# Low parts by negative copies and accumulating DMAs, and one plain tile fewer in each up-projection

## The chip, the cores and the metric

The kernel runs on one core of a Trainium2 chip. The metric is the device time in microseconds, the median of several runs; a profiled execution is read beside it. Lines are written L198 for line 198 of the kernel before.

## The reference

One layer on x of 512 tokens by 1024 channels, all in float32:

```
x = x + 0.5 * (silu(h @ w_gate) * (h @ w_up)) @ w_down      # h = rmsnorm(x), d_ff = 2816
x = x + mixer(rmsnorm(x))                                    # chunked attention and pooling
x = x + 0.5 * (silu(h @ w_gate) * (h @ w_up)) @ w_down      # second FFN, own weights
x = rmsnorm(x)
```

The change touches only the up-projections (gate and up) of the two FFNs.

## The kernel before

**Numbers in two parts.** Every float32 operand z is split into a high part, z rounded to the matmul's format (fp32r), and a low part z - high, which is rounded in its turn. `split` (L128) makes them: ScalarE copies (L132, or L135 with a scale), VectorE subtracts (L133, or L136 with a scale). A product is then three matmuls (`mm3`, L198 to L200): high by high, high weights by low tokens, low weights by high tokens. The third is the only one that reads the low part of the weights.

**The up-projection** (`ffn_up`) goes over 22 tiles of 128 hidden channels, gate and up each. It has three kinds of stages.

- The first stage takes tiles 0 and 1 together, over four chunks of weights, while the norm is still under way. At its end stands the norm's mean on TensorE (L334), then Ln and Exp on ScalarE, and two passes on VectorE (L324, L328) that give rb, the factor of each token.
- Plain tiles: 2 to PLAIN - 1. Each has two weight tiles of 128 by 1024 (`weights`, loads at L181 on SyncE's queue, split by `split`) and 2 x 8 `mm3` with 512 columns, 48 matmuls. `evacuate` (L418 gate times rb, L420 silu on ScalarE, L422, then L725 in `place` for up times that, and L732 and L733 in `sums` for every second one of a pair) empties the two banks. PLAIN is 5 in the first FFN and 4 in the second.
- Seven-product tiles: from PLAIN to 21. Tokens and weights are taken as 2 by 2 blocks, and the Winograd form of Strassen's scheme makes the tile from seven products of half the columns (4 `mm3` each, 84 matmuls with 256 columns), in the order A11, S3, S2, A22, S1, A12, S4 of the token operands. Their order on TensorE, VectorE and ScalarE is written out by hand. The weight operands are sums of blocks (L494, L500, L501), again in two parts (L471 and L476), called w11, w13, w24 and w22. S3 and A22 use halves of w13 and w24 (S and on), S2 the first half of w24, A12 and S4 w22.

**The way into the seven-product tiles.** The token operands have to exist by the first of these tiles. `Norm.blocks` gives a list of 19 pieces of work, which `piece` hands out: eight scalings of x by gain and rb (L359), sums of blocks (L365), and the splits: S3 and S2 (`whole`, with sign -1, so L135 and L136), S4 (`whole`, L132 and L133), and A11, A22, S1 and A12 (`halves`, two half operands each, 512 columns, into the rooms in which the norm's h lay, so only when the last plain tile has read them). The plain tiles before the last get four pieces after each weight tile; before the last one all but four pieces are handed out; the last plain tile gets the remaining four: A11 after its second step, A22 after the fourth, S1 after the sixth, and A12 at the end, after the evacuation. The last plain tile alternates between its two banks at every step and carries the preparation of the first seven-product tile in between. The order of plain tiles and pieces on TensorE, VectorE and ScalarE is a scheduler's, by readiness and then by place in the code.

**GpSimd's queue.** `Down.make_sums` copies one column of a given tile (mark, L714), which ties it to that tile's progress, and then issues DMAs in DRAM (L716, some of them accumulating) that make the weight sums of the down-projection. A region `manual_schedule` keeps the order of the instructions inside it on its engine; where a region falls among others is the scheduler's. In the second FFN, x is also put aside from here (L935).

**Rooms.** Parts of weights have four rooms in turn, raw weights two and two; a room is given again when its last reader is done.

Of the kernel before, what the change touches and what calls it, by code (L numbers as in the profile page):

```python
# [11 lines left out]
AF = mybir.ActivationFunctionType  # L12
ALU = mybir.AluOpType
# [3 lines left out]
P = 128  # L17
D = 1024
S = 512
KD = D // P  # L20
# [14 lines left out]
RAW = 2  # L35
HILO = 3
SHIFT = 16
PLAIN = (5, 4)
PROBS = 3
EARLY = 16  # L40
LATE = 4
# [4 lines left out]
    weights=(-1.0, 0.905, 3.0), qk=2.0, turn=1.1, head=0.9, pool=0.965, map=0.95, u=2.0,  # L46
# [10 lines left out]
def layer(  # L57
# [31 lines left out]
    nc = tc.nc  # L89
# [28 lines left out]
    A11, S1, S3, S2, A12, A22, S4 = range(7)  # L118
# [10 lines left out]
    def split(src, hi, lo, scale=None):  # L129

        if scale is None:
            nc.scalar.copy(hi, src)  # L132
            nc.vector.tensor_tensor(lo, src, hi.bitcast(F32), op=ALU.subtract)  # L133
        else:
            nc.scalar.activation(hi, src, AF.Copy, scale=scale)  # L135
            nc.vector.scalar_tensor_tensor(  # L136
                lo, src, scale, hi.bitcast(F32), op0=ALU.mult, op1=ALU.subtract
            )


    rooms: list = [(wpool, "raw", RAW, 1024)]
    n_raw = [0]

# [28 lines left out]

    n_own = [0]

    def weights(src, parts=1):
        n = src.shape[-1]
        raw = raw_tile()
        hi, lo = part_tiles()
        for i in range(parts):
            part = slice(i * n // parts, (i + 1) * n // parts)  # L180
            nc.sync.dma_start(raw[:, part], src[:, part])  # L181
            split(raw[:, part], hi[:, part], lo[:, part])
        return hi, lo

    def ordered(acc):
# [7 lines left out]
    def mm3(acc, a, b, start, stop, further=False):  # L193

        more = dict(skip_group_check=True) if further else {}
        acc = acc.rearrange("p (i a) -> p i a", a=2)
        high, low = (z.rearrange("p (a i) -> p i a", a=2) for z in b)
        nc.tensor.matmul(acc, a[0], high, start=start, stop=False, **more)  # L198
        nc.tensor.matmul(acc, a[0], low, start=False, stop=False, **more)  # L199
        nc.tensor.matmul(acc, a[1], high, start=False, stop=stop, **more)  # L200

    def cut(pair, lo, n):
        return pair[0][:, lo : lo + n], pair[1][:, lo : lo + n]
# [80 lines left out]
    class Norm:  # L284
# [57 lines left out]
        def blocks(self, pool, aside):  # L342

            x_lo, x_hi = (z[:, : 4 * S].rearrange("p (k c) -> p k c", c=S) for z in aside[:2])
            a11, a21 = x_lo[:, :, :HT], x_lo[:, :, HT:]  # L350
            a12, a22 = x_hi[:, :, :HT], x_hi[:, :, HT:]
            s2, s4, s1 = (
                z[:, at : at + 4 * HT].rearrange("p (k c) -> p k c", c=HT)
                for z, at in ((aside[0], 4 * S), (aside[1], 4 * S), (aside[2], 0))
            )
            self.a = [None] * 7

            def scale(k):
                nc.vector.scalar_tensor_tensor(  # L359
                    (x_lo, x_hi)[k // 4][:, k % 4], x[k], gain_sb[:, self.which, k : k + 1],  # L360
                    self.rb, op0=ALU.mult, op1=ALU.mult,
                )

            def add(dst, one, two, op):
                nc.vector.tensor_tensor(dst, one, two, op=op)  # L365

            def whole(i, src, make, sign=None):
                pair = [make().rearrange("p (k c) -> p k c", c=HT) for _ in range(2)]
                split(src, *pair, sign)
                self.a[i] = [[z[:, k] for k in range(4)] for z in pair]  # L370

            def halves(i, src):

                self.a[i] = [[], []]
                for k in (0, 2):
                    pair = [
                        hpool.tile([P, 2, HT], F32R, tag="h", name=name("ha")) for _ in range(2)
                    ]
                    split(src[:, k : k + 2], *pair)
                    for z, to in zip(pair, self.a[i]):  # L380
                        to.extend(z[:, j] for j in range(2))

            def by_x(i):
                return lambda: xpool.tile([P, 2 * S], F32R, tag=f"x{i.pop()}", name=name("xa"))

            def extra():
                z = pool.tile([P, 4 * HT + 64], F32R, tag="extra", name=name("sa"), bufs=2)
                return z[:, 48 : 48 + 4 * HT]

            free = [3, 2, 1, 0]  # L390
            return [(scale, k) for k in range(KD)] + [
                (add, s1, a21, a22, ALU.subtract),
                (add, s2, s1, a11, ALU.add),
                (add, a21, a11, a21, ALU.add),
                (whole, S3, a21, by_x(free), -1.0),
                (whole, S2, s2, by_x(free), -1.0),
                (add, s4, s2, a12, ALU.subtract),
                (whole, S4, s4, extra),
                (halves, A11, a11),
                (halves, A22, a22),  # L400
                (halves, S1, s1),
                (halves, A12, a12),
            ]


    def ffn_up(norm, wA, down, loaded, in_order, plain, turns=()):
# [9 lines left out]
        def evacuate(f, gate, up):  # L416
            g = temp()
            nc.vector.tensor_tensor(natural(g), ordered(gate), natural(norm.rb), op=ALU.mult)  # L418
            sg = temp()
            nc.scalar.activation(sg, g, AF.Silu)  # L420

            nc.vector.tensor_tensor(sg, sg, norm.rb, op=ALU.mult)  # L422
            down.place(f, ordered(up), sg)
            down.sums(f)
            return sg
# [89 lines left out]
        def low24(n):  # L515
            if n < KF:
                low((n, 24))

        for n, f in enumerate(down.order[2 : plain - 1], 2):
            banks = []  # L520
            for j in range(2):
                wj = weights(wA[2 * f + j])
                acc = bank()
                for k in range(KD):
                    mm3(acc, cut(wj, k * P, P), norm.h[k], k == 0, k == KD - 1)
                banks.append(acc)
                piece(4)
            down.make_sums(evacuate(f, *banks))
        piece(len(todo) - 4)

        n, f = plain - 1, down.order[plain - 1]
        wj = [weights(wA[2 * f + j]) for j in range(2)]
        banks = [bank(), bank()]
        fetch(plain)
        for k in range(KD):
            for j in range(2):
                mm3(banks[j], cut(wj[j], k * P, P), norm.h[k], k == 0, k == KD - 1)
            if k == 1:
                high11(plain)
                low11(plain)  # L540
                piece()
            elif k == 3:
                fetch(plain + 1)
                sum13(plain)
                high13(plain)
                low13(plain)
                piece()
            elif k == 5:
                sum24(plain)
                piece()  # L550
# [1515 lines left out]
```

## Time and profile before

| | |
|---|---|
| median of 3 runs | 804.68 us (804.41 to 805.51) |
| profiled execution | 804.5 us, span 802.7 us |
| granted TensorE clock, mean | 0.998 |
| first stage, first FFN | 4.8 to 28.4 us |
| plain tiles, first FFN | 28.42 to 60.26 us (three) |
| seven-product tiles, first FFN | from 60.26 us |
| plain tiles, second FFN | 505.70 to 526.50 us (two) |
| seven-product tiles, second FFN | from 526.50 us |

PE is TensorE, PEld its loads of weights, DVE VectorE, ACT ScalarE, POOL GpSimd, SP SyncE. In the rows of a timeline stand the start, the length, the engine, the line, the operation, what it writes and reads, and its shape; in brackets the idle time before it and what ended it. Matmuls and VectorE's passes overlap a little with the next one, so the distance from start to start is what one costs. In rows of waits the engine and line that waited come first, then whom it waited for, the total, the number of times and the longest.

### The profile page before, as it was taken

Reading aid. Unit: us, or ns where it says so; the run is one execution under the profiler, and the core shown is the slowest. Engines: PE = TensorE matmul, PEld = TensorE weight load, DVE = VectorE, ACT = ScalarE, POOL = GpSimd, SP = SyncE. Lnnn points to the kernel's source line nnn. Section 1 sums busy time; section 2 is a strip of 40 time slices with the busy share of each in tenths; the row PEclk is TensorE's granted clock in tenths of the full one; section 3 lists DMA queues with packets and bytes.
Section 4 is the critical chain, followed back from the end, with each engine's and each line's share of the span. In section 5 each row is a group of like instructions: output and inputs, shape, how many; then the busy total and the mean of one; then the engine's idle time right before and its main releaser. Section 6 shows DMA issues by size and latency. Waiting matters only on the chain.

```text
span 802.7 us, 14916 instructions
## 1 busy us (share of the span) xinstructions
PE 793.5 (99%) x5706; PEld 745.4 (93%) x5706; DVE 709.3 (88%) x1112; ACT 499.7 (62%) x857; POOL 152.5 (19%) x240
## 2 busy tenths in 40 slices
PE   9999999999999999999999999999999999999996
PEld 7889999999999999888888888899999999988986
DVE  7999999999987997778789688999999999986997
ACT  8456655556675675559769545455666655766584
POOL 0023212223220000231444263101110011200010
PEclk9999999999999999999999999999999999999999
DMA  8266889879999675585764867236666457869642
GB/s 291 77 210 210 239 229 245 216 187 259 241 293 317 220 212 156 183 255 100 189 197 81 185 155 204 105 115 205 168 160 195 159 171 175 259 238 343 210 141 105
DMA packets 73848, 158.57 MB, mean 198 GB/s; under 512 B 6560, under 2 KB 31664, under 8 KB 73392
## 3 DMA queue, kind: packets, MB, share of 16 engines
q1 hardware_dynamic: 49808, 109.09, 40.2%
q0 software_dynamic: 23680, 48.24, 28.5%
q8 instruction: 45, 0.74, 0.4%
q10 hardware_dynamic: 288, 0.27, 0.1%
q14 instruction: 27, 0.22, 0.1%
HBM read 153.38 MB, written 50.34 MB: 254 GB/s over the span
## 4 chain that ended last, share of the span: by engine, by line
PE 89%; DVE 5%; issue 1%; DMA 1%; ACT 1%; SPq 0%; DVEq 0%; ACTq 0%
PE mm L200 18%; PE mm L198 18%; PE mm L199 18%; PE a L198 11%; PE a L199 11%; PE a L200 10%; DVE aside L359 1%; PE mm L1528 1%; DVE parts L133 1%; PE mm L1592 1%; DMA raw<-in_wA_dram 1%; DVE aside L365 1%; PE a L1618 1%; PE mm L1618 1%; PE a L1592 0%
## 5 line engine op out<-in xcount | busy, mean ns | idle before, releaser
L565 ACT ACTIVATE t<-mm 128x256 f32<-128x256 f32 x105 | 40.5, 386 | 112.0 <-PE mm L200 110.0
L132 ACT CAST parts<-raw 128x1024 fp32r<-128x1024 f32 (+2 forms) x77 | 74.1, 968 | 51.4 <-PE mm L199 16.6
L133 DVE TENSOR_TENSOR parts<-raw,parts 128x1024 fp32r<-128x1024 f32 (+2 forms) x77 | 85.7, 1121 | 14.8 <-ACT parts L132 14.1
L714 POOL COPY mark<-t 128x1 f32<-128x1 f32 x40 | 16.4, 410 | 331.4 <-DVE t L609 247.7
L199 PE MATMUL mm<-ha,parts 128*128 128x256 f32 x280 | 77.0, 275 | 0.0
L200 PE MATMUL mm<-ha,parts 128*128 128x256 f32 x280 | 77.0, 275 | 0.0
L198 PE MATMUL mm<-ha,parts 128*128 128x256 f32 x280 | 77.0, 275 | 0.0
L716 POOL DMA_DIRECT2D wsum<-in_wB_dram x72 | 70.7, 1114 | 22.5 <-DMA wsum<-wsum 15.0
L476 DVE TENSOR_TENSOR parts<-wsum,parts 128x1024 fp32r<-128x1024 f32 x53 | 64.5, 1218 | 5.1 <-ACT parts L471 5.1
L471 ACT CAST parts<-wsum 128x1024 fp32r<-128x1024 f32 x53 | 53.8, 1046 | 0.8 <-DVE wsum L494 0.4
L198 PEld LDWEIGHTS mm<-ha,parts 128*128 128x128 f32 x280 | 53.8, 192 | 0.1
L199 PEld LDWEIGHTS mm<-ha,parts 128*128 128x128 f32 x280 | 53.8, 192 | 0.1
L200 PEld LDWEIGHTS mm<-ha,parts 128*128 128x128 f32 x280 | 53.8, 192 | 0.0
L133 DVE TENSOR_TENSOR ah<-acts,ah 128x512 fp32r<-128x512 f32 (+1 forms) x72 | 47.1, 662 | 3.0 <-ACT ah L132 2.9
L200 PE MATMUL mm<-hhi,parts 128*128 128x512 f32 x120 | 45.9, 385 | 0.5 <-DVE parts L133 0.5
L198 PE MATMUL mm<-hhi,parts 128*128 128x512 f32 x120 | 45.4, 382 | 0.7 <-DVE t L418 0.3
L199 PE MATMUL mm<-hlo,parts 128*128 128x512 f32 x120 | 46.0, 385 | 0.0
L132 ACT CAST ah<-acts 128x512 fp32r<-128x512 f32 (+1 forms) x72 | 40.8, 580 | 8.3 <-PE mm L199 6.4
L476 DVE TENSOR_TENSOR parts<-raw,parts 128x512 fp32r<-128x512 f32 (+1 forms) x52 | 43.4, 858 | 0.0
L494 DVE TENSOR_TENSOR wsum<-raw 128x1024 f32<-128x1024 f32 x35 | 42.6, 1218 | 0.0
L1116 ACT CAST parts<-raw 128x1024 fp32r<-128x1024 f32 x24 | 25.1, 1046 | 25.8 <-DMA raw<-in_wQK_dram 6.0
L471 ACT CAST parts<-raw 128x512 fp32r<-128x512 f32 (+1 forms) x52 | 39.2, 754 | 2.9 <-DMA raw<-in_wA_dram 2.9
(332 smaller groups left out, 3066.5 us busy)
## 6 DMA issues: line engine op xcount, KB each, us to landing
raw<-in_wA_dram SPq DMA_DIRECT2D x87, 512.0 KB, 4.5
wsum<-in_wB_dram POOLq DMA_DIRECT2D x60, 512.0 KB, 6.9
raw<-wsum SPq DMA_DIRECT2D x36, 512.0 KB, 5.1
raw<-in_wB_dram SPq DMA_DIRECT2D x30, 512.0 KB, 4.7
wsum<-wsum POOLq DMA_DIRECT2D x20, 512.0 KB, 4.5
x<-in_xT_dram SPq DMA_DIRECT2D x16, 256.0 KB, 6.2
raw<-in_wQK_dram SPq DMA_DIRECT2D x8, 512.0 KB, 4.0
wsum<-in_wB_dram POOLq DMA_DIRECT2D x12, 256.0 KB, 6.9
```

The lines of the kernel that those rows point to most:

```text
L132: nc.scalar.copy(hi, src)
L133: nc.vector.tensor_tensor(lo, src, hi.bitcast(F32), op=ALU.subtract)
L198: nc.tensor.matmul(acc, a[0], high, start=start, stop=False, **more)
L199: nc.tensor.matmul(acc, a[0], low, start=False, stop=False, **more)
L200: nc.tensor.matmul(acc, a[1], high, start=False, stop=stop, **more)
L471: nc.scalar.copy(hi, src)
L476: nc.vector.tensor_tensor(lo, src, hi.bitcast(F32), op=ALU.subtract)
L494: nc.vector.tensor_tensor(z, raw[:, : 2 * S], raw[:, S : 3 * S], op=ALU.add)
L565: nc.scalar.activation(natural(dst), ordered(src), AF.Copy, scale=scale)
L714: nc.gpsimd.tensor_copy(mark[:, 0:1], after[:, 0:1])
L716: nc.gpsimd.dma_start(self.rows(i, g), self.rows(self.terms[i][at], g), **(dict(accum_op=ALU.add) if at else {}),)
L1116: return lambda: nc.scalar.copy(buf["part", i][0], buf["raw", i])
```

## The change

A second way to make the two parts: ScalarE writes the high part and then the negative copy of the source, rounded like the high part, into the low part's room, and a DMA from GpSimd's queue adds the source to it. VectorE has no part in it. It is used for the weights of the plain tiles, for S4, and for A12. S3 and S2 (with a sign), A11, A22, S1, the first stage's weights, the weights of the seven-product tiles and those of the down-projections keep the old way.

PLAIN goes from (5, 4) to (4, 3): tile 4 of the first FFN and tile 3 of the second become seven-product tiles, and the second FFN is left with one plain tile, which is also its last.

The plain weights are loaded and split one tile ahead (`plain_weights`), and the DMAs for the sums of a plain tile are given out one tile later, after the next tile's weights.

```diff
-PLAIN = (5, 4)
+PLAIN = (4, 3)
...
+    def split_by_dma(src, hi, lo):
+
+        nc.scalar.copy(hi, src)
+        nc.scalar.activation(lo, src, AF.Copy, scale=-1.0)
+        with tc.manual_schedule(engines={mybir.EngineType.Pool}):
+            nc.gpsimd.dma_start(lo, src, accum_op=ALU.add)
...
-    def weights(src, parts=1):
+    def weights(src, parts=1, by_dma=False):
...
-            split(raw[:, part], hi[:, part], lo[:, part])
+            (split_by_dma if by_dma else split)(raw[:, part], hi[:, part], lo[:, part])
...
             def whole(i, src, make, sign=None):
...
-                split(src, *pair, sign)
+                if sign is None:
+                    split_by_dma(src, *pair)
+                else:
+                    split(src, *pair, sign)
...
-            def halves(i, src):
+            def halves(i, src, by_dma=False):
...
-                    split(src[:, k : k + 2], *pair)
+                    (split_by_dma if by_dma else split)(src[:, k : k + 2], *pair)
...
-                (halves, A12, a12),
+                (halves, A12, a12, True),
...
+        def plain_weights(n):
+            return [weights(wA[2 * down.order[n] + j], by_dma=True) for j in range(2)]
+
+        ahead, done = plain_weights(2), None
         for n, f in enumerate(down.order[2 : plain - 1], 2):
             banks = []
+            now, ahead = ahead, plain_weights(n + 1)
+            if done is not None:
+                down.make_sums(done)
             for j in range(2):
-                wj = weights(wA[2 * f + j])
                 acc = bank()
                 for k in range(KD):
-                    mm3(acc, cut(wj, k * P, P), norm.h[k], k == 0, k == KD - 1)
+                    mm3(acc, cut(now[j], k * P, P), norm.h[k], k == 0, k == KD - 1)
                 banks.append(acc)
                 piece(4)
-            down.make_sums(evacuate(f, *banks))
+            done = evacuate(f, *banks)
         piece(len(todo) - 4)

         n, f = plain - 1, down.order[plain - 1]
-        wj = [weights(wA[2 * f + j]) for j in range(2)]
+        wj = ahead
         banks = [bank(), bank()]
         fetch(plain)
+        if done is not None:
+            down.make_sums(done)
```

## Prediction

> **What bounds the kernel now.** I read the page's table of engines first, then the waits of TensorE.
>
> ```profile
> PE 793.5 (99%) x5706; PEld 745.4 (93%) x5706; DVE 709.3 (88%) x1112; ACT 499.7 (62%) x857; POOL 152.5 (19%) x240
> PE mm L200 <- DVE parts L133: 0.5, 1, 0.5
> PE a L334 <- DVE acc L305: 0.4, 1, 0.4
> PE mm L198 <- DVE t L418: 0.3, 1, 0.3
> ```
>
> TensorE is busy for 99% of the span, so time is won only by giving it less to do or by removing the few waits it has. The three largest waits that this change can touch all lie in the short stretches where an up-projection goes over from plain tiles to seven-product tiles, and all three are for VectorE. So the next view is the busy time by stretch: the way into the seven-product tiles of the first and of the second FFN, and between them a stretch of seven-product tiles alone.
>
> ```profile
> 26.80:62.10 35.30, 34.81 (x170) 30.33 (x169) 35.28 (x49) 16.73 (x24) 6.88 (x6) 1.00 0.39 120
> 74.00:210.00 136.00, 136.00 (x1220) 136.00 (x1220) 127.03 (x180) 80.64 (x144) 32.40 (x48) 1.00 0.89 231
> 494.90:528.30 33.40, 33.07 (x162) 28.88 (x161) 33.13 (x44) 16.02 (x22) 5.12 (x6) 1.00 0.32 96
> ```
>
> After the length come the busy times of PE, PEld, DVE, ACT and POOL, then the granted clock (1.00) and the DMA share. In both ways in, VectorE is busy for the whole stretch (35.28 of 35.30, 33.13 of 33.40), while ScalarE is half idle and DMA is at 0.39 and 0.32. Later VectorE needs 127.03 of 136.00, 93%, so a backlog is worked off slowly. Near the start of each FFN, VectorE is therefore as tight as TensorE.
>
> **What TensorE gains.** The timeline of TensorE gives the length of a tile.
>
> ```profile
> 28.42 0.38 PE L198 MATMUL mm<-hhi,parts 128*128 128x512 f32 x1
> 49.14 0.38 PE L198 MATMUL mm<-hhi,parts 128*128 128x512 f32 x1
> 60.26 0.27 PE L198 MATMUL mm<-ha,parts 128*128 128x256 f32 x1
> 69.81 0.28 PE L198 MATMUL mm<-ha,parts 128*128 128x256 f32 x1
> 210.51 0.28 PE L198 MATMUL mm<-ha,parts 128*128 128x256 f32 x1
> 504.99 0.38 PE L200 MATMUL mm<-hhi,wlo 128*128 128x512 f32 x1
> 505.70 0.45 PE L198 MATMUL mm<-hhi,parts 128*128 128x512 f32 x1 [0.33 <-DVE t L418]
> 526.50 0.27 PE L198 MATMUL mm<-ha,parts 128*128 128x256 f32 x1
> ```
>
> Plain tiles 2 and 3 of the first FFN run from 28.42 to 49.14: 10.36 us each, 0.216 per matmul (48 in a tile). Fifteen seven-product tiles run from 69.81 to 210.51: 9.38 us each, 1.34 per product. A plain tile that becomes a seven-product tile saves 0.98 us, the two of them 1.96. Plain tile 4 takes 60.26 - 49.14 = 11.12, so 0.76 of it is waiting; 505.70 comes 0.71 after the matmul before it, 0.49 more than 0.216; and 0.4 goes at L334. If VectorE bound nothing, the gain would be 1.96 + 0.76 + 0.49 + 0.4 = 3.6 us.
>
> **What VectorE must do by then.** The timeline of VectorE gives the distances between starts, the beginning of each way in, and its end.
>
> ```profile
> 19.97 1.22 DVE L133 TENSOR_TENSOR parts<-raw,parts 128x1024 fp32r<-128x1024 f32 x1
> 21.11 0.68 DVE L305 TENSOR_TENSOR acc<-acc,t 128x512 f32<-128x512 f32 x1
> 26.82 0.75 DVE L359 SCALAR_TENSOR_TENSOR aside<-x,gain_sb,rb 128x512 f32<-128x512 f32 x1
> 42.06 0.42 DVE L732 TENSOR_TENSOR acts<-acts 128x256 f32<-128x256 f32 x1
> 42.40 1.22 DVE L136 SCALAR_TENSOR_TENSOR xa<-aside,xa 128x1024 fp32r<-128x1024 f32 x1
> 60.30 0.68 DVE L418 TENSOR_TENSOR t<-mm,rb 128x512 f32<-128x512 f32 x1
> 60.90 1.21 DVE L476 TENSOR_TENSOR parts<-wsum,parts 128x1024 fp32r<-128x1024 f32 x1
> 62.04 0.68 DVE L133 TENSOR_TENSOR ha<-aside,ha 128x512 fp32r<-128x512 f32 x1
> 493.05 1.21 DVE L133 TENSOR_TENSOR parts<-raw,parts 128x1024 fp32r<-128x1024 f32 x1
> 494.18 0.68 DVE L328 SCALAR_TENSOR_TENSOR rb<-t,t 128x512 f32<-128x512 f32 x1
> 494.89 1.41 DVE L359 SCALAR_TENSOR_TENSOR aside<-x,gain_sb,rb 128x512 f32<-128x512 f32 x2
> 527.05 1.22 DVE L476 TENSOR_TENSOR parts<-wsum,parts 128x1024 fp32r<-128x1024 f32 x1
> ```
>
> One pass costs 0.34 (42.06 to 42.40), 0.60 (60.30 to 60.90) or 1.14 (60.90 to 62.04) for 256, 512 or 1024 columns. The way in opens with the first scaling (L359), as soon as the factor rb (L328) exists, and what matters at its end is the low part of w24 (L476 at 60.90 and 527.05): product S2, third in the tile, reads it in its third matmul, 2 x 1.34 + 0.22, say 2.95 us, after the tile's start.
>
> First FFN, before: 62.04 - 26.82 = 35.2 us without a gap, ready 1.2 before the 63.2 at which it is needed. From these 35.2 fall: three low parts of plain weights (3 x 1.14), the low part of S4 (1.14), that of the first half of A12 (0.60), and the evacuation of one plain tile with its sums (3 x 0.60 + 2 x 0.34): 7.6 in all. 27.6 stay. The low pass at 19.97 goes too; it stood ahead of L305, on which the norm waits, so rb can come up to 1.1 earlier. Negative copies on ScalarE, which that norm also needs, can eat this up; I take 0.6, a start at 26.2. w24 is then ready at 53.8. TensorE reaches its first seven-product tile at 49.14 - 0.4 = 48.7, when the old tile 4 began, and needs w24 at 51.7: a new wait of 2.1 us. One seven-product tile more stands behind it, so the old point corresponds to 53.8 + 9.4 = 63.2: no change.
>
> Second FFN, before: from 494.89 to 527.05 + 1.14 = 528.2, 33.3 us. Here fall three low parts of weights (3.4), S4 (1.14), half of A12 (0.60) and the three passes of one evacuation (1.8): 6.9. 26.4 stay. The pass at 493.05 stands between rb and its predecessor, so rb comes up to 1.1 earlier; I take 0.9, a start at 494.0, and w24 at 520.4. TensorE ends the first stage at 505.2, its one plain tile at 515.6, and needs w24 at 518.5: a wait of 1.9. 520.4 + 9.4 = 529.8 against 526.50 + 2.95 = 529.45: 0.3 later.
>
> In both I counted L418 ahead of w24, as at 60.30; with VectorE behind it may as well fall after it, 0.6 less each. I take half, -0.6 together. Sum: 0.0 + 0.3 - 0.6 = -0.3 us. The two tiles and the old waits give 3.6, and nearly all of it goes back as two new waits of 1.5 to 2 us for w24.
>
> **What the DMAs and the rest cost.** The nearest rows for an accumulating DMA from SBUF to SBUF are other transfers on GpSimd's queue, the nearest for a negative copy an ACTIVATE with a scale.
>
> ```profile
> L135 ACT ACTIVATE xa<-aside 128x1024 fp32r<-128x1024 f32 x2 | 2.1, 1058 | 2.2 <-DVE aside L365 2.2
> wsum<-in_wB_dram POOLq DMA_DIRECT2D x60, 512.0 KB, 6.9
> wsum<-wsum POOLq DMA_DIRECT2D x20, 512.0 KB, 4.5
> x_d<-t POOLq DMA_DIRECT2D x8, 64.0 KB, 4.0
> 492.25 5.13 POOL L935 DMA_DIRECT2D x_d<-t  x8 [7.94 <-DVE t L928]
> 38.20 2.25 POOL L714 COPY mark<-t 128x1 f32<-128x1 f32 x1 [36.40 <-DVE t L422]
> 63.45 1.04 POOL L714 COPY mark<-t 128x1 f32<-128x1 f32 x1 [10.67 <-DVE t L422]
> 64.93 1.24 POOL L716 DMA_DIRECT2D wsum<-in_wB_dram  x1
> 68.72 0.24 POOL L714 COPY mark<-t 128x1 f32<-128x1 f32 x1 [2.54 <-DVE t L609]
> 529.45 0.51 POOL L716 DMA_DIRECT2D wsum<-wsum  x1
> ```
>
> A landing takes between 4.0 and 6.9 us; I take 4.5, the copy of the same size. It cannot turn out a gain beyond the VectorE passes already counted, since nothing else is removed. The tightest plain weights are those of the second FFN: GpSimd is through with x_d at 492.25 + 5.13 = 497.4, issues two DMAs of 0.5 to 1.1 each, and they land at 502.4 to 506.5, where TensorE reads the low parts at 505.6 and 506.3. By the middle value they are hidden; at the far end 0.2 us shows, which disappears in the wait for w24. The first FFN prefetches with over 4 us to spare. Each negative copy is 1.06 on ScalarE, at most five more in a way in where it is busy 16.73 of 35.30: hidden beside VectorE, except ahead of rb, where I have charged it. The loads of plain weights move one tile ahead on SP, past the loads of the first seven-product tile, and hold their raw room some 3 us longer; SP has no wait of TensorE behind it there. The sums for the down stage (mark, L714) start up to a tile later; the down stage reads them after 220 us. The fifteen pieces now sit ahead of the one plain tile instead of between tiles; their VectorE passes are in the chain above. The GpSimd DMA is a new wait on that queue, for ScalarE's negative copy; behind it stand only marks and sums.
>
> **Rivals.** First, VectorE's order spares TensorE: the passes of A22 and S1 (four of 0.60, needed a product or more after w24) are put behind w24. 2.4 less covers both waits of 2.1 and 1.9, and up to the full 3.6 us is kept: 801.1 to 802.7, about 801.9. Against it: before, all four stood ahead of w24, and they are earlier in the code.
>
> Second, slower: A12's low parts get stuck on GpSimd. In the code their DMAs come after the mark and the sums of the last plain tile. Before, that mark began at 63.45, 3.2 after the first seven-product tile, and its second DMA was issued at 64.93 and would land 6.9 later, at 71.8, 11.6 after the tile's start; A12, the sixth product, is read 6.8 after it. If A12's DMAs stand behind, TensorE waits 4.8 us in the first FFN; in the second 529.45 + 4.5 + two issues of 0.5 is 8.4 after 526.50, 1.6 late. Together +6.4: 810.7. It decides when the evacuation's L422 is done before ScalarE's second negative copy of A12, some 2 us into the tile; with VectorE behind, the mark is late and A12 should go first.
>
> Third, GpSimd's issue is slowed by a busy VectorE: the mark at 38.20 took 2.25 where VectorE had no gap, 0.24 at 68.72. Two more us for each issue put A12's second half at 1.3 + 2 x 2.6 + 4.5 = 11.0 after the tile's start, against 7.5 plus the wait of 2: 1.5 late in each FFN, +3.0, 807.3. Against it: eight x_d issues took 0.64 each beside a full VectorE. The Trainium skill, SBUF — State Buffer, "Who interferes with whom", states that a VectorE instruction with two SBUF inputs and a GpSimd instruction that reads SBUF block each other, and "SBUF: two separate sides" that descriptors of GpSimd's DMAs starve during VectorE's two-port modes, which tensor_tensor has not; by the first rule this rival would hold only for the marks, and the x_d issues agree.
>
> **The numbers.** The profiled execution took 804.5 (span 802.7) beside a median of 804.68; I add the difference of -0.3 to the median: 804.3 us, chance 0.50. Its own range: the starts of the chains by -0.6 and +0.6, -0.3 and +0.9, the place of L418 by 0.6 either way, so 802.9 to 806.4. First rival 0.24, second 0.15, third 0.11. About 0.2%, 1.6 us, is what a measurement can tell from no change. Faster: all of the first rival and 0.11 of my case, 0.35. Slower: 0.08 of my case, 0.15, and 0.08 of the third, 0.31. The same: 0.34. The range runs from 801.3, near the first rival's end, to 808.0, above the third; it leaves out the second.
>
> **What would show it.** Right: in the waits of TensorE two new entries for VectorE's L476, in the third product of the first seven-product tile, 1 to 2.5 us each; that tile begins near 48.7 and 515.6; no wait at L334; VectorE full from rb to w24, some 27 us long. Wrong: no such waits (first rival); a wait for a DMA of a ha tile at the sixth product (second or third, told apart by the mark standing ahead of it or by issues over 2 us); or a wait for parts in plain tiles.

## The result and the profile after

The changed kernel takes 835.61 us (median of 5 runs) against 804.58 us of the kernel before beside it: 31 us longer, ratio 1.0391 (95% interval 1.0373 to 1.0409). The profiled execution took 838.77, 3 above the median, span 837.0, against 804.5 and 802.7: 34.3 of span are to be found. Lines have moved: `mm3` is L206 to L208, the mean L342, rb L336, the sums of blocks L373, the evacuation L429, L431, L433 and L744, the parts of the seven-product weights L482 and L487, the copies of the products' accumulators L584, the mark L733 and its DMAs L735. L143, L144 and L146 are the new split: high copy, negative copy, DMA.

First the page's table of engines, then the waits of TensorE (total, times, longest):

```profile
PE 802.5 (96%) x5778; PEld 753.6 (90%) x5778; DVE 707.4 (85%) x1112; ACT 515.6 (62%) x883; POOL 160.0 (19%) x252
```

```profile
PE mm L207 <- DMA ha<-aside: 10.1, 1, 10.1
PE mm L207 <- DVE parts L1140: 7.0, 1, 7.0
PE mm L206 <- DVE t L429: 3.3, 3, 1.7
PE mm L206 <- ACT t L584: 3.1, 2, 2.2
PE mm L206 <- ACT parts L132: 1.9, 3, 1.0
PE mm L206 <- DVE parts L487: 0.7, 1, 0.7
PE a L342 <- DVE acc L313: 0.3, 1, 0.3
```

Before, no wait in the stretches that the change touches was over 0.5. Now there are two long ones. The first is A12's low part (ha) in the first seven-product tile. The second, L1140, is the low part of the mix's first weights, 260 us after anything that the diff touches in the first FFN. Then come waits of 1 to 2 us for evacuations (L429) and for ScalarE (L584, L132). They add up to some 26; the rest is in the view of stretches (the length, then the busy times of PE, PEld, DVE, ACT and POOL, then the granted clock):

```profile
56.00:58.00 2.00, 2.00 (x11) 1.87 (x10) 2.00 (x4) 1.75 (x4) 1.32 (x2) 0.50 0.00 0
71.50:75.50 4.00, 4.00 (x19) 4.00 (x20) 1.26 (x2) 0.00 (x0) 0.00 (x0) 0.50 0.77 120
343.00:352.00 9.00, 4.99 (x12) 3.99 (x13) 5.34 (x8) 3.29 (x5) 0.00 (x0) 0.50 0.32 115
537.00:543.00 6.00, 5.29 (x14) 3.95 (x13) 5.72 (x9) 1.32 (x3) 0.00 (x0) 0.50 0.31 59
```

The clock, 1.00 before until the last 3 us of the kernel, is 0.50 in four stretches, each behind a wait: 19 matmuls of 256 columns take 4.00 us, 0.21 each instead of 0.112. It stays so for 3.4, 10, 10 and 7 us, of which TensorE works about 3.3, 4.5, 5.7 and 5.4 and so loses half: 9 to 10 us. Waits and clock make some 36; less the 2 that the tiles bring and about 1 of old waits that went, that is some 33 of the 34.3.

Where A12 was late, in GpSimd's timeline, with the DMA view of 55 to 73 us below it (KB each, and median us from issue to landing):

```profile
56.68 1.11 POOL L733 COPY mark<-t 128x1 f32<-128x1 f32 x1 [6.95 <-DVE t L433]
57.74 1.94 POOL L735 DMA_DIRECT2D wsum<-in_wB_dram  x2
59.04 3.10 POOL L146 DMA_DIRECT2D ha<-aside  x2
```

```profile
wsum<-in_wB_dram POOLq DMA_DIRECT2D x3, 512.0 KB, 11.1
ha<-aside POOLq DMA_DIRECT2D x2, 256.0 KB, 12.6
```

The mark came first, its two sums went out, and A12's two DMAs only after them; they landed 12.6 us after issue, behind those sums (11.1). TensorE stood from 61.2 to 71.4. In the second FFN A12's DMAs were ahead of the mark (550.67 and 553.18 against 553.90), took 3.7 to land, and nobody waited for them.

In the second FFN the evacuation of the first stage stands behind the pieces on VectorE:

```profile
531.07 1.22 DVE L373 TENSOR_TENSOR aside<-aside,aside 128x1024 f32<-128x1024 f32 x1
532.21 1.22 DVE L136 SCALAR_TENSOR_TENSOR xa<-aside,xa 128x1024 fp32r<-128x1024 f32 x1
533.34 0.68 DVE L429 TENSOR_TENSOR t<-mm,rb 128x512 f32<-128x512 f32 x1
533.94 1.21 DVE L136 SCALAR_TENSOR_TENSOR xa<-aside,xa 128x1024 fp32r<-128x1024 f32 x1
535.08 0.68 DVE L433 TENSOR_TENSOR t<-t,rb 128x512 f32<-128x512 f32 x1
535.68 0.68 DVE L429 TENSOR_TENSOR t<-mm,rb 128x512 f32<-128x512 f32 x1
```

TensorE was through with the first stage at 532.5; the passes that free its banks (L429) began at 533.34 and 535.68, with passes of 1.2 ahead of and between them. VectorE has no gap here.

### The profile page after: what moved, and what is told of

Its sections match the earlier page's. It is cut to its first block, busy times and chain, and to the rows that moved or that the text cites. A ratio compares the mean times of both kernels' runs of the same rounds, so it can differ in the third digit from the quotient of the medians.

```text
span 837.0 us, 15114 instructions
## 1 busy us (share of the span) xinstructions
PE 802.5 (96%) x5778; PEld 753.6 (90%) x5778; DVE 707.4 (85%) x1112; ACT 515.6 (62%) x883; POOL 160.0 (19%) x252
## 4 chain that ended last, share of the span: by engine, by line
PE 83%; DVE 7%; DMA 4%; issue 2%; ACT 2%; SPq 0%; POOL 0%; DVEq 0%; ACTq 0%
PE mm L207 17%; PE mm L206 16%; PE mm L208 16%; PE a L206 10%; PE a L207 10%; PE a L208 10%; DMA raw<-in_wA_dram 3%; DMA ha<-aside 1%; DVE aside L367 1%; DVE aside L373 1%; PE mm L1547 1%; PE mm L1611 1%; PE a L1637 1%; PE mm L1637 1%; DVE parts L487 1%
## 5 line engine op out<-in xcount | busy, mean ns | idle before, releaser
L584 ACT ACTIVATE t<-mm 128x256 f32<-128x256 f32 x111 | 42.8, 385 | 116.6 <-PE mm L208 114.7
L487 DVE TENSOR_TENSOR parts<-wsum,parts 128x1024 fp32r<-128x1024 f32 x74 | 90.2, 1219 | 11.3 <-ACT parts L482 11.3
L133 DVE TENSOR_TENSOR parts<-raw,parts 128x1024 fp32r<-128x1024 f32 (+2 forms) x71 | 78.8, 1117 | 15.8 <-ACT parts L132 14.5
L132 ACT CAST parts<-raw 128x1024 fp32r<-128x1024 f32 (+2 forms) x71 | 67.8, 962 | 36.2 <-PE mm L207 9.4
L206 PE MATMUL mm<-ha,parts 128*128 128x256 f32 x296 | 81.7, 276 | 0.7 <-DVE parts L487 0.7
L208 PE MATMUL mm<-ha,parts 128*128 128x256 f32 x296 | 81.4, 275 | 0.0
L207 PE MATMUL mm<-ha,parts 128*128 128x256 f32 x296 | 81.4, 275 | 0.0
L735 POOL DMA_DIRECT2D wsum<-in_wB_dram x72 | 70.3, 1110 | 21.8 <-DMA wsum<-wsum 13.7
L482 ACT CAST parts<-wsum 128x1024 fp32r<-128x1024 f32 x74 | 73.8, 1046 | 0.0
L733 POOL COPY mark<-t 128x1 f32<-128x1 f32 x40 | 13.5, 338 | 284.7 <-DVE t L628 270.5
L206 PEld LDWEIGHTS mm<-ha,parts 128*128 128x128 f32 x296 | 56.9, 192 | 1.4 <-ACT ha L132 1.4
L207 PEld LDWEIGHTS mm<-ha,parts 128*128 128x128 f32 x296 | 56.8, 192 | 0.1
L208 PEld LDWEIGHTS mm<-ha,parts 128*128 128x128 f32 x296 | 56.8, 192 | 0.0
L207 PE MATMUL mm<-ha,whi 128*128 128x256 f32 x148 | 41.5, 280 | 10.1 <-DMA ha<-aside 10.1
L132 ACT CAST ah<-acts 128x512 fp32r<-128x512 f32 (+1 forms) x72 | 40.8, 580 | 10.4 <-PE mm L207 7.1
L487 DVE TENSOR_TENSOR wlo<-raw,whi 128x1024 fp32r<-128x1024 f32 x37 | 45.0, 1217 | 0.2 <-ACT whi L482 0.2
L206 PE MATMUL mm<-xa,parts 128*128 128x256 f32 x148 | 41.3, 279 | 3.1 <-ACT t L584 3.1
L1140 DVE TENSOR_TENSOR parts<-raw,parts 128x1024 fp32r<-128x1024 f32 x24 | 29.2, 1222 | 16.6 <-ACT parts L1135 16.6
L206 PE MATMUL a<-ha,parts 128*128 128x256 f32 x148 | 41.3, 279 | 0.4 <-ACT t L584 0.4
```

Source lines behind the costliest of these rows:

```text
L584: nc.scalar.activation(natural(dst), ordered(src), AF.Copy, scale=scale)
L735: nc.gpsimd.dma_start(self.rows(i, g), self.rows(self.terms[i][at], g), **(dict(accum_op=ALU.add) if at else {}),)
L1140: nc.vector.tensor_tensor(lo, buf["raw", i], hi.bitcast(F32), op=ALU.subtract)
```

## The experiments

Four theories were tried. A: A12's DMAs stood behind the sums on GpSimd. B: the wait at the mix comes from the rooms of weight parts that fell out of step, since the first FFN now takes 80 pairs of parts instead of 78 (4 for the first stage, 2 for a plain and 4 for a seven-product tile) and four rooms go round. C: idle time of TensorE halves its clock. D: the banks of the second FFN. Against them stands that the accumulating DMAs as such, ScalarE's load, or the fewer plain tiles cost it. The loads one tile ahead and the later sums stay in all runs but those made from the kernel before; no run takes them alone.

**A12 by the old split.**

```diff
-                (halves, A12, a12, True),
+                (halves, A12, a12),
```

> The changed kernel with one part undone: A12's two low parts are made by VectorE again; all other low parts stay with the accumulating DMAs, and there are four and three plain tiles. Theory A (A12's accumulating DMAs stand in order behind the sums of the down weights on GpSimd's queue): the wait of 10.2 us for the ha tile in the first FFN goes, and with it the 2.3 us lost to the halved clock behind it; VectorE gets two passes of 0.60 more, of which up to 1.2 shows at S2. 835.6 - 12.5 + 0.6 = about 824 (822 to 826); the other losses (the start of the mix, the second FFN) stay. Rival R (A12's place on the queue is a symptom: the added negative copies on ScalarE, or the fewer plain tiles, hold the first seven-product tile up anyway): TensorE waits there for something else, and at most 4 us are won, 831 or more.

Measured: 825.54, 10.1 less. The wait for ha is gone, nothing took its place in that tile, and the wait at S2 is the same 2.2. The 10 us belong to A12's new way; whether to its place on GpSimd or to the way itself, the next run tells.

**A12's DMAs ahead of the sums.**

```diff
-        down.make_sums(evacuate(f, *banks))
-        piece()
+        sg = evacuate(f, *banks)
+        with tc.manual_schedule(engines={mybir.EngineType.Pool}):
+            piece()
+            down.make_sums(sg)
```

> The changed kernel with one order changed: the accumulating DMAs of A12 go to GpSimd ahead of the mark and the two sums of the last plain tile, not behind them. Theory A: they are issued as soon as ScalarE's copies are done (57.5), two issues of about 2 us each, and land 4 to 6 us after issue, at 62 to 65 instead of 71.4 and 72.7; TensorE needs them at 61.1, so a wait of 1 to 4 us stays and about 8 of the 12.5 us are won: about 827 (824 to 830). Rival R2 (an accumulating DMA from SBUF to SBUF takes some 12 us in this stretch wherever it stands, because the other transfers slow it): the landing stays near 70, and the time within 2 us of 835.6. What is made is the same in both.

Measured: 831.67, 3.9 less, half of what was expected. (The two profiled executions lie 8.0 apart, but that of the changed kernel also has the halved clock behind S2, which this one has not.) The waits of TensorE and the DMA view:

```profile
PE mm L207 <- DMA ha<-aside: 4.1, 2, 2.4
```

```profile
ha<-aside POOLq DMA_DIRECT2D x2, 256.0 KB, 6.9
```

The landing fell from 12.6 to 6.9 and the wait from 10.1 to 4.1, so the order was most of the wait, and theory A holds. The two issues took until 59.2 all the same, and A12's copies come off ScalarE at 56.5 and 57.5 for a need at 61 to 62: even first in the queue, this DMA is too late here. Behind its two waits the clock was halved from 64.0 to 70.8.

**The rooms put back in step.**

```diff
-    n_parts = [0]
+    n_parts = [2]
...
-    n_own = [0]
+    n_own = [2]
```

> The changed kernel with the two counters that choose the rooms of the weight parts started at 2 instead of 0, so that the mix and the down projection find the same rooms as in the kernel before (the first FFN takes 80 pairs of parts instead of 78, and rooms rotate by 4). Theory B (the loss of 9.9 us at the start of the mix comes from rooms that fell out of step): the wait of 7.3 us for the parts of the mix's first weights goes, and the 2.6 us of halved clock behind it: 835.6 - 9.9 = about 826 (824 to 828). Rival (the mix starts late because ScalarE or VectorE lag behind from the first FFN, or because its weights are loaded late): within 2 us of 835.6.

Measured: 822.95, 12.7 less. The wait at the mix is gone, and with it waits of 1.0 and 1.5 and the halved clock in the second FFN, which I had not counted. The same edit in the kernel before, with no other change:

> The kernel before with nothing changed but the start of the two counters of rooms (2 instead of 0), so that the rooms are now out of step at the start of the mix. Theory B: the wait of some 7 us for the parts of the mix's first weights appears in the kernel before, with 2 to 5 us of halved clock behind it and the knock-on in the second FFN: 804.6 + 10 to 12.7 = 814 to 817. Rival (the rooms cost only with the lateness of the changed first FFN): 804 to 806.

Measured: 816.47, 11.7 longer than 804.77, ratio 1.0143 (1.0130 to 1.0157). ScalarE's copies of the mix's weights, first in the kernel before, then in that kernel:

```profile
316.56 1.05 ACT L1116 CAST parts<-raw 128x1024 fp32r<-128x1024 f32 x1 [1.43 <-PE a L199]
319.24 1.05 ACT L1116 CAST parts<-raw 128x1024 fp32r<-128x1024 f32 x1 [1.63 <-PE a L199]
322.40 1.04 ACT L1116 CAST parts<-raw 128x1024 fp32r<-128x1024 f32 x1 [2.12 <-DMA raw<-in_wQK_dram]
```

```profile
322.20 1.05 ACT L1116 CAST parts<-raw 128x1024 fp32r<-128x1024 f32 x1 [7.32 <-PE a L199]
327.99 1.03 ACT L1116 CAST parts<-raw 128x1024 fp32r<-128x1024 f32 x1
```

In step, two weights of the mix are copied and a third is begun while the down-projection still runs (TensorE reaches the mix at 323.2). Out of step, the first copy waits 7.32 us for the last reader of its room and starts only at 322.20. In the changed kernel the same copy waited the same 7.32. Nothing but where the count starts differs here, so theory B is shown from both sides.

**Fewer plain tiles without the DMAs** (the changed kernel, low parts all by VectorE; PLAIN (4, 3), the loads one tile ahead and the later sums stay).

```diff
-                if sign is None:
-                    split_by_dma(src, *pair)
-                else:
-                    split(src, *pair, sign)
+                split(src, *pair, sign)
...
-                (halves, A12, a12, True),
+                (halves, A12, a12),
...
-            return [weights(wA[2 * down.order[n] + j], by_dma=True) for j in range(2)]
+            return [weights(wA[2 * down.order[n] + j]) for j in range(2)]
```

> The kernel before with the fewer plain tiles alone (four and three) and the loads one tile ahead; every low part is made by VectorE, no accumulating DMA is left. If the accumulating DMAs are what costs (rival R3), this kernel lies near 804 to 806. By my account of VectorE, w24 of the first seven-product tile is ready at 57 in the first FFN against a need at 51.7 and at 524 against 518.5 in the second: two waits of about 5.5 us, less the 3.6 that the tiles and old waits give; the wait at the start of the mix stays (rooms, theory B, 9.9), and each wait costs some 2 to 4 us more by the halved clock (theory C): 804.6 + 11 - 3.6 + 9.9 + 4 to 8 = 826 to 830. Without theory C 822, without theory B 812 to 820.

Measured: 823.6, 2.4 under the forecast's range; the two waits that it put at 5.5 each were 2.7 and 2.1. With the rooms in step as well:

> Fewer plain tiles (four and three) with all low parts by VectorE, no accumulating DMA, and the rooms started two further on. Theory B: against the same kernel without that start it loses the wait at the start of the mix with its clock, 823.6 - 10 to 12.7 = 811 to 814. Against the run that has both edits (810.7) the difference is what the accumulating DMAs of the plain weights and of S4 bring once A12 is left to VectorE: by the work they take from VectorE ahead of w24 (3.4 us in each FFN) up to 3 us, so 811 to 814 too. Rival (the DMAs bring nothing, since the copies that they need go to a full ScalarE): 809 to 811.

Measured: 814.11, ratio 1.0114 (1.0100 to 1.0128). So without any accumulating DMA the fewer plain tiles, with the loads ahead, cost 9 us with the rooms right. TensorE waits 2.7 for VectorE's low parts of weight operands in the first FFN, and 3.5 in the second for ScalarE's copy of a product's accumulators (L581 here, L584 in the changed kernel): both engines come late to the first seven-product tile.

**Both edits at once.**

> The changed kernel with both edits at once: A12's low parts by VectorE, and the rooms of the weight parts started two further on. If the two losses are separate (theories A and B), their gains of 10.1 and 12.7 us add up: 835.6 - 22.8 = about 813 (811 to 815). Rival (the wait at the start of the mix and the one in the first FFN hide one another, or one lateness causes both): 818 or more.

Measured: 810.72, ratio 1.0077 (1.0053 to 1.0101): 24.9 less than the changed kernel, a little more than 10.1 + 12.7. The two losses are separate. Against the run without DMAs (814.11) the DMAs of the plain weights and of S4 bring some 3, though the two intervals just touch (1.0053 to 1.0101 and 1.0100 to 1.0128). What is left is 6 us. The three longest entries of an execution of 813.66 are S2 in the first FFN, the banks in the second, and two short waits in later seven-product tiles:

```profile
PE mm L206 <- ACT t L584: 2.2, 1, 2.2
PE mm L206 <- DVE t L429: 2.2, 3, 1.7
PE a L206 <- ACT t L584: 1.4, 2, 0.7
```

**Four plain tiles in the second FFN** (the kernel with both edits, PLAIN (4, 4)).

> As the kernel with both edits, but four plain tiles in the second FFN too, so that the tile behind its first stage asks for one bank at a time and not for two within 0.65 us. Theory D (the waits of 2.05 and 1.09 us at 522.3 and 524.6 come from banks of the first stage that VectorE has not yet read out, because the tile behind it is the interleaved one): these waits go, one plain tile costs 0.98 more, and the wait of 1.2 for w24 becomes shorter: 2 to 3 us under the kernel with both edits, about 810.5. Rival (VectorE is late there however the banks are asked for): the waits stay and the time is some 1 us above that kernel.

Measured: 813.87, 3.1 above the kernel with both edits. Behind the first stage there are waits of about 1 each for ScalarE's copies of the next weights (L132, L143), for L744 and for L429, and the clock is halved from 513.1 to 519.9. The waits for banks (L429, L744) still make 1.7 instead of 2.2, so that two banks are asked for at once is at most a small part of it; that form of theory D falls.

**The DMAs alone** (PLAIN back to (5, 4)).

> The accumulating DMAs alone: five and four plain tiles as before, and the low parts of the plain weights, of S4 and of A12 by negative copies and accumulating DMAs. There are 78 pairs of parts in the first FFN again, so by theory B no wait at the start of the mix; by theory D no wait for banks in the second FFN. By theory A A12 still stands behind the sums of the last plain tile: TensorE needs it at 67 in the first FFN, and it lands some 12 us after an issue near 65: a wait of 8 to 10 and 2 of halved clock: 804.6 - 1.6 + 10 to 12 = 813 to 815. Rival (the DMAs are harmless where VectorE has a tile more to work with, and only the fewer plain tiles cost): 802 to 805.

Measured: 814.69, ratio 1.0124 (1.0109 to 1.0140): the number as expected, for the wrong reason. A12's DMAs were issued ahead of the mark (62.52 and 64.50 against 65.59), and no wait for them is left. TensorE waits 2.2 for a plain weight's low part from its DMA, and in the second FFN for ScalarE, which is full behind the new copies:

```profile
508.53 1.04 ACT L143 CAST sa<-aside 128x1024 fp32r<-128x1024 f32 x1
509.48 1.05 ACT L144 ACTIVATE sa<-aside 128x1024 fp32r<-128x1024 f32 x1
510.44 0.61 ACT L431 ACTIVATE t<-t 128x512 f32<-128x512 f32 x1
510.96 1.03 ACT L143 CAST whi<-raw 128x1024 fp32r<-128x1024 f32 x1
```

TensorE came to the weight whose high part is copied at 510.96 some 1.1 us before it was there. Ahead of it on ScalarE stand both copies of S4, which nobody needs before 546. The clock is then halved from 513.3 to 520.1. In the profiled execution (816.5) the mix begins 4.4 us later than before, and the second FFN adds some 7.

**One DMA alone, S4's, in the kernel before.**

> The kernel before with one accumulating DMA in each FFN: the low part of S4 alone is made by a negative copy and a DMA; five and four plain tiles, all else by VectorE. VectorE has 1.14 us less to do ahead of w24 in each FFN, ScalarE 1.05 more, and nobody needs S4 soon. If an accumulating DMA is a fair price where it does not load ScalarE at a busy time: 804.6 less at most 0.7 (of the old waits of 0.76 and 0.49), so 804 to 804.6. Rival (any shift of VectorE's and ScalarE's order at this place costs more than it frees, as in the run with the DMAs alone): 806 or more.

Measured: 804.39 against 804.77, ratio 0.9994 (0.9986 to 1.0003): no difference. The last plain tile of the first FFN takes 10.36 instead of 11.12, as expected, but the mix begins at 323.27 against 323.17: given back on the way. It is the only one of these kernels with an accumulating DMA that isn't slower.

**Idle time put in by hand** (the kernel before, with small copies on ScalarE ahead of the copy for which S2 waits, in eight tiles).

```diff
+                for _ in range(DELAY[loaded].get(n, 0)):
+                    nc.scalar.copy(probe, probe)
                 copy(u[:, :HT], acc)
```

> The kernel before with small copies of an unused tile added on ScalarE, ahead of the copy for which product S2 waits, in four tiles of each FFN (12, 20, 32, 56 and 16, 26, 42, 72 copies of some 0.1 to 0.2 us): TensorE stands idle for eight known lengths, from under 1 to some 10 us, with nothing else changed. Theory C (an idle TensorE is what halves its clock): after the short ones the granted clock stays at 1.00, after those of more than some 2 us it is 0.50 for 3 to 10 us, in steps of about 3.4. Rival (the halved clock in the changed kernel comes from the load of the DMAs or of the other engines, not from idle time): 1.00 throughout, and the time is longer by the idle time alone.

Measured, in a single run: 877.54, span 875.5, 72.8 longer than before. The eight waits, and stretches behind the first, the second (twice) and the last of them:

```profile
PE mm L199 <- ACT t L568: 56.1, 8, 15.8
```

```profile
93.60:97.60 4.00, 4.00 (x36) 4.00 (x37) 3.50 (x6) 1.09 (x3) 0.00 (x0) 1.00 0.82 270
126.00:129.00 3.00, 3.00 (x16) 3.00 (x16) 2.88 (x4) 0.69 (x3) 0.00 (x0) 0.50 0.75 281
129.30:140.00 10.70, 10.70 (x98) 10.70 (x97) 7.98 (x13) 5.58 (x10) 2.52 (x3) 1.00 0.71 117
721.30:726.40 5.10, 5.10 (x24) 5.10 (x25) 3.21 (x4) 0.99 (x3) 0.00 (x0) 0.50 0.01 3
```

After 1.71 us of idle time the clock stayed at 1.00. After 2.65 and 3.59 it was 0.50 for 3.4 us, after 5.0 and 6.4 for 6.8, after 8.8 and 12.1 for 10.2, after 15.8 for 17.1; the longer stretches begin within the wait itself. The waits sum to 56.1, which leaves 16.7. In the halved stretches TensorE worked for some 30 us; half of that, about 15, is lost to the clock, some 2 for each of the seven waits behind which it was halved. Theory C holds: only idle time was added.

**What is left: the order on VectorE and ScalarE.** In the second FFN the two gate passes of the first stage are written out in order behind eleven pieces, on the kernel with both edits (`gated` is an evacuation's L429 and L431, and `evacuate` then does the rest of it):

```diff
+            with tc.manual_schedule(engines={mybir.EngineType.DVE}):
+                piece(11)
+                sgs = gated(first[0]), gated(first[2])
+            evacuate(0, first[0], first[1], sgs[0])
+            evacuate(1, first[2], first[3], sgs[1])
```

> As the run with both edits, but in the second FFN VectorE's order is written out: eleven of the fifteen pieces, then the two gate passes of the first stage (L429) back to back, then the rest; there L136 and L433 stood between the two passes, 1.74 us. Theory D2 (VectorE's fixed order, with long passes of the pieces between the passes that free banks, causes the waits of 2.05 and 1.09 us, and these the halved clock of 3.4 us behind them): 1.7 of wait and 1.7 of clock go, 810.7 - 3 = about 807.5 (806 to 809). Rival (ScalarE or the sum of VectorE's work is late there in any order): within 1.5 of 810.7.

Measured: 811.67, no gain. A long pass (L136), which the region doesn't hold, still fell between the two, and the wait of 1.7 went over to the bank that L754, the last pass of the evacuation (L744 before the edit), frees. For the first FFN, the first plain tile's parts were given back to VectorE:

```diff
-            return [weights(wA[2 * down.order[n] + j], by_dma=True) for j in range(2)]
+            return [weights(wA[2 * down.order[n] + j], by_dma=loaded or n > 2) for j in range(2)]
```

> As the run with both edits, but in the first FFN the first plain tile's two weights get their low parts from VectorE; the later plain tiles, the second FFN and S4 keep the DMAs. Theory S (the negative copies on ScalarE, which stand ahead of the norm's three steps, hold up the factor rb by 2 us in the first FFN, and with it VectorE's whole chain to w24; VectorE itself is idle for 5.5 us just ahead of rb, so the two passes cost nothing there): rb comes 1.3 to 2 earlier, the wait of 2.5 at S2 shrinks to about 1, and below 2 us the clock stays whole (1.7): 810.7 - 3 = about 807.5 (806.5 to 809.5). Rival (ScalarE's copies behind rb, or the sum of VectorE's work, set w24 and the copy ahead of S2): within 1.2 of 810.7.

Measured: 810.98 against 810.72: the rival holds. rb comes 0.6 earlier (26.88 against 27.49), the whole chain with it, and so does TensorE; S2 waits the same 2.2. Then, on that kernel, the second FFN's order to the end, all of both evacuations ahead of the last four pieces:

```diff
             with tc.manual_schedule(engines={mybir.EngineType.DVE}):
                 piece(11)
                 sgs = gated(first[0]), gated(first[2])
+                evacuate(0, first[0], first[1], sgs[0])
+                evacuate(1, first[2], first[3], sgs[1])
+                piece(4)
```

> As that kernel, and in the second FFN VectorE's order is written out to the end: eleven pieces, both gate passes, the rest of both evacuations, and only then the last four of the fifteen pieces (in the earlier attempt at this order one long pass still fell between the gate passes and a second ahead of the pass that frees the next bank). Theory D2 (the long passes between those that free banks cause the bank waits): the waits of 1.1 and 1.7 us seen there go, and the 1.7 of halved clock behind them; 2 to 4 less than the kernel without this order: about 804.5 (803 to 806). Rival (VectorE's work is late there in any order, so that what the banks win w24 loses in the first seven-product tile): within 1.5 of the kernel without this order.

Measured: 826.06, 15 longer, by the mechanism of theory A again. GpSimd's timeline in the second FFN:

```profile
502.14 0.94 POOL L146 DMA_DIRECT2D parts<-raw  x1 [0.60 <-issue]
521.03 0.86 POOL L146 DMA_DIRECT2D sa<-aside  x1 [17.95 <-ACT sa L144]
521.60 1.17 POOL L146 DMA_DIRECT2D parts<-raw  x1
```

The edit put S4's DMA (sa) ahead of one of the plain tile's; that one stood 18 us behind S4's copies, and TensorE waited 14.0 for it. With S4's piece left out of the order (`piece(3)`):

> As the kernel with VectorE's order written out in the second FFN, but the piece of S4 is left out of that order and comes after the plain tile's weights, so that its accumulating DMA stands behind theirs on GpSimd (in the run before, one of theirs stood behind S4's and was issued 19.5 us later, which cost a wait of 14.0). Theory D2: the bank waits of 2.0 and 1.1 us are gone as in that run, nothing new comes, and 2 to 4 us are won against 811: 807 to 809. Rival (what the banks win w24 loses in the first seven-product tile): 810 to 812.

Measured: 812.73, ratio 1.0104 (1.0088 to 1.0120). The waits of TensorE:

```profile
PE mm L206 <- ACT t L595: 4.8, 2, 2.6
PE mm L206 <- ACT ha L132: 1.6, 1, 1.6
```

No bank is waited for any more, so the bank waits do come from VectorE's order. But TensorE now waits 1.6 for ScalarE's copy of A11 (0.7 before this order) and 2.6 at S2 in the second FFN too (L595 is the copy L584 of the changed kernel). What the banks win is lost there: the rival holds, 0.7 above its range. No version here beats the kernel before, and of the last 6 us the parts are seen in the waits, but no run takes them away.

## Why the prediction was wrong

The forecast was 0.3 us less; 31 more were measured. The two edits that put A12 and the rooms right take away 24.9 of them, so the main failures are a wait that the prediction held unlikely and a term that its sum does not have.

- **VectorE's chain: length right, start wrong.** In the first FFN it was to last 27.6 us, from 26.2 to 53.8. It ran without a gap from 28.21 to 55.34, 27.1 us, but rb came at 27.41, not at 25.5. ScalarE's copies for the new split stood among the three steps of the norm (L326, L327, L328), where I had charged 0.6; in the run without any DMA and the rooms in step, rb came at 25.99 with all of VectorE's passes in place.

```profile
21.48 1.06 ACT L144 ACTIVATE parts<-raw 128x1024 fp32r<-128x1024 f32 x1
22.66 0.69 ACT L326 ACTIVATE t<-a,eps 128x512 f32<-128x512 f32 x1
23.52 1.05 ACT L143 CAST parts<-raw 128x1024 fp32r<-128x1024 f32 x1 [0.17 <-PE mm L207]
24.47 0.72 ACT L327 ACTIVATE t<-t,less_ln 128x512 f32<-128x512 f32 x1
25.09 1.04 ACT L144 ACTIVATE parts<-raw 128x1024 fp32r<-128x1024 f32 x1
26.04 0.61 ACT L328 ACTIVATE t<-t 128x512 f32<-128x512 f32 x1
```

- **The wait at S2: its length right, the engine only in part.** 2.1 was forecast, for VectorE's low part of w24 (L487, L476 before):

```profile
54.93 0.38 PE L206 MATMUL mm<-xa,parts 128*128 128x256 f32 x1 [2.22 <-ACT t L584]
54.20 1.22 DVE L487 TENSOR_TENSOR parts<-wsum,parts 128x1024 fp32r<-128x1024 f32 x1
```

TensorE waits 2.22 for ScalarE's copy L584, and two matmuls later another 0.2 for w24's low part. So VectorE would have caused such a wait by itself, but ScalarE, "half idle" on average, was gapless from 46.5 to 57.7 and nearly as late. That the length fits is partly luck: w24 was ready 1.5 later than forecast, and TensorE came to the tile 1.1 later (49.84, not 48.7). In the second FFN, where 1.9 was forecast, ScalarE's copy holds S2 up by 2.6 once the banks are out of the way; in the changed kernel they stand ahead of it.
- **A12: the step that failed most directly.** The second rival described this wait and had a chance of 0.15, because of one sentence: "With VectorE behind, the mark is late and A12 should go first." The point from which it decides was named rightly, the evacuation's pass against ScalarE's second negative copy. But the copy came off ScalarE at 57.5 and the mark went at 56.68. In the second FFN A12 did go first. The price was also too low: 4.8 in this FFN was worked out with the sums' landing of 6.9; A12's own DMAs took 12.6, and the wait was 10.1.
- **The pieces.** "Their VectorE passes are in the chain above" counts their sum and not their place: the first stage's evacuation stands among them, and TensorE needs its banks at once. In the second FFN that cost some 4 us of waits (3.1 for L429, 0.7 for L487) and about 2.7 of clock, and writing the order out only moved the wait on to ScalarE and S2.
- **The rooms.** No step looked at what goes round by a count. The two tiles turned into seven-product ones changed the count by 2 in each FFN. That is the largest single term, 12 us, and lies where the diff changes nothing.
- **The clock.** Each wait was priced at its length, with a granted clock of 1.00 read from stretches without waits. Behind the longer waits some 2 each came on top, 9 to 10 in all.
- **Right:** the plain weights' DMAs in the changed kernel landed in 5.6 to 6.0 in the first FFN (median of a group), within the 4.0 to 6.9, and TensorE waited for none. The wait at the mean (L342) stays at 0.3, against the forecast.

## What to carry to other kernels

Price a moved step by its place on each in-order queue, not by the engine's average: a DMA issue inherits everything ahead of it on GpSimd, a cheap copy everything on ScalarE. Count what goes round (rooms, banks) whenever a change adds or drops a user, and look at the next stage's first use of it. And if TensorE has no gaps now, a new gap can cost more than its length: in these runs some 2 us of halved clock on top, where it left TensorE idle for more than half of a step of 3.4 us.

## What the runs showed of the hardware

The granted clock is 1.00 or 0.50, and its halved stretches last 3.4 us or a multiple of it (3.4, 6.8, 10.2, 17.1 in the run with idle time). The Trainium skill, TensorE: Matmul & The Clock Gate, "What's actually happening", states that the clock is halved after an idle window of about 3.4 us and released after a busy one, and that the windows run free of the program. The steps agree; but a single wait of 2.65 was enough here, as was the one of 2.2 at S2 in the changed kernel, and in others of these runs the same 2.2 at the same place left the clock at 1.00.

The traces show what decides. In all 17 profiled executions the clock changes only at whole multiples of 3.413 us from its first change. Of these steps, at full clock, 51 ended in a halving, and TensorE was busy for 0.47 or less of each; where it stayed full TensorE was busy for 0.50 or more, but for two steps (0.43 and 0.45) near the end of a kernel. So the measurement is wider than an idle window: a step in which TensorE idles for a little over half is enough. The 2.2 at S2 falls into one step in the changed kernel (first row, 1.14 busy of 3.41; the clock is halved from 55.50 on), and is shared by two in the kernel with both edits, where the clock stays:

```profile
52.09:55.50 3.41, 1.14 (x9) 0.76 (x7) 3.41 (x6) 3.39 (x7) 0.00 (x0) 1.00 0.21 41
50.41:53.82 3.41, 2.38 (x22) 2.19 (x20) 3.41 (x6) 3.40 (x6) 0.00 (x0) 1.00 0.77 150
53.82:57.24 3.42, 2.18 (x17) 1.99 (x18) 3.42 (x6) 3.23 (x8) 0.47 (x1) 1.00 0.00 0
```

Where the steps begin differs from execution to execution (the first change lies 4.3 us after the start in the first of these and 6.0 in the second); no run here sets it.

A12's two DMAs of 256 KB, issued behind two of 512 KB, landed 12.6 us after their issue (median); issued ahead of them at the same place they took 6.9, and 3.7 in the second FFN. The Trainium skill, DMA: Bandwidth & Descriptors, "Queues, rings and completion order", states of DMAs issued by SP and ACT that the semaphore's increment lands only after every earlier write from the same DMA engine. The rows, of DMAs issued by GpSimd, would agree with the same for these; no run here tells it apart from plain queueing for the same engines.
